# The opening stage of a decoder-trunk kernel: GpSimd subtractions moved, some work given to ScalarE and TensorE, a repacked modulation weight, a new order

## The chip, the cores and the metric

One Trainium2 chip, one core of it. The metric is the device time of one execution in microseconds (us). Every time below is either such a time or is read from one profiled execution. The engines are called by the profile's names: PE is TensorE (PEld its weight loads), DVE is VectorE, ACT is ScalarE, POOL is GpSimd, SP is SyncE, which here only issues transfers (SPq).

## What is computed

One decoder layer on 512 tokens of width 1024. The part that matters here is its beginning: a modulation vector from the condition `c`, a normalised and modulated input `h`, and the first projections of `h`.

```python
c_act = silu(c)
mod = c_act @ w_mod + b_mod                       # w_mod: 1024 x 6144
sh1, sc1, gt1, sh2, sc2, gt2 = split(mod, 6)
h = rms_norm(x, g_norm1) * (1 + sc1) + sh1        # x: 512 x 1024
proj = h @ w_in                                   # then gMLP, GLA, sparse attention, w_out
x = x + gt1 * mixer(proj)
h2 = rms_norm(x, g_norm2) * (1 + sc2) + sh2
out = x + gt2 * hier_moe(h2)                      # top-1 group, top-2 experts in it
```

Products are made to near-f32 accuracy from two parts: each operand is split into a high part (rounded to the fp32r type) and a low part (the operand minus its high part), and three products are added: high x high, high x low, low x high.

## The kernel before

The opening stage is everything up to the moment when the first six 128-column blocks of `w_in` have been multiplied with all of `h`. It is written out by hand as a list of steps, the string `START`. The loop over that string calls one small function for each word, so the string sets the order of the instructions on every engine; each engine then runs its own instructions strictly in that order and waits at the first one whose input is missing.

The width 1024 is cut into eight columns dc = 0 to 7 of 128. The words are, with the function that each calls:

- `Lx` (`load_xt`), `Lm` (`load_mod`), `Lu` (`first_load`): transfers, issued by SP in this order: four 128-token tiles of `x`; for each column a 1 MB piece of `w_mod` (the two 128-column pieces for the shift `sh1` and the scale `sc1`) in two transfers of 512 KB; six weight units of 512 KB, `raw`. There are four buffers for `w_mod` pieces and three for `raw`; a load whose buffer is still in use waits on SP, and all later loads wait behind it.
- `sq`, `rs`, `sc` (`x_sq`, `x_rstd`, `x_norm`): ACT squares a token tile and sums it, DVE and POOL make the reciprocal root, DVE scales the tile.
- `xt`, `xs`, `xe` (`x_t`, `x_evac`): PE transposes the tile in 128 x 128 pieces (`xs7` does the last column), and ACT or DVE copies a finished column out of PSUM into `xnT`.
- `mp`, `ma`, `mb` (`mod_products`, `mod_sums`): the modulation of a column. Partition p holds eight rows k = 0 to 7 of `w_mod`. ACT multiplies two of them with `c_act` into `mpg`; DVE adds the other six in two interleaved chains `macc` (SCALAR_TENSOR_TENSOR, 128 x 256 each) and joins the chains in one addition.
- `mo`, `mc` (`mod_column`, `mod_scale`): PE sums `macc` over the partitions by a product with a column of ones; DVE makes scale and shift `mc` of the column.
- `hh`, `hf`, `hl` (`h_hi`, `h_full`, `h_lo`): the modulated column. ACT writes its high part `hTh`; `hf` writes the full row in f32; `hl` subtracts to give the low part `hTl`. The letter in `hl0G` is the engine: V is DVE, G is POOL.
- `wh`, `wl` (`first_hi`, `first_lo`): high part (ACT) and low part (DVE or POOL, by the letter) of a weight unit; the low part of units 0 to 3 is `wlo`, of units 4 and 5 `mg`.
- `f` followed by unit, column and part (`first_c`): one product, 128 x 512. Each of the six units has 8 columns x 3 parts, so 144 products. Part 0 is hTh with the high weights, part 1 hTh with the low ones, part 2 hTl with the high ones.
- `wm` with a number (`warm`): that many dummy products on PE.

In the kernel before, the subtractions `wl0` to `wl3`, `wl5` (`wl4` is on DVE) and `hl0`, `hl1`, `hl4`, `hl6`, `hl7` carry the parts that are named G or V in the string; five of the weight subtractions and five of the `hl` subtractions run on POOL. After `START` come the next units (`gk`, then `av`), whose splits are ACT and DVE work, and then the rest of the layer, which is the same text in both kernels.

Of the kernel before, what the change touches and what calls it, by code (L numbers as in the profile page):

```python
# [38 lines left out]
LV = [1, 2, 4, 8, 16, 32, 64]  # L39

START = """
Lx0 Lx1 sq0 Lx2 rs0 sq1 Lx3 sc0 rs1 wm9 xt0 sq2 Lm0 sc1 rs2 sq3 xt1 sc2 rs3 xt2 Lu0 sc3 mp0 wm3 xt3 Lm1 ma0 xs7 xe0A
mb0 wh0 xe1A wl0G xe3A Lu1 xe4A xe2V wm10 mo0 mp1 mc0 Lm2 hf0 hh0 ma1 wh1 hl0G wm7 f000 mb1 f001 xe5A f100 xe7A wl1G
f102 f002 Lu2 xe6V mo1 mp2 mc1 Lu3 hf1 hh1 ma2 wm4 f101 wh2 hl1G f110 mb2 Lm3 f111 f010 f011 f200 f210 wh3 wl2G f202
f112 f212 f012 mo2 f300 mc2 f310 f302 Lu4 hf2 f312 hh2 wl3G f201 f211 mp3 hl2V f320 f120 f220 f121 ma3 f221 f322 Lu5
wh4 f020 f122 mb3 f301 f311 f321 f222 Lm4 f400 f410 f402 f420 f412 wh5 wl4V f021 mo3 f422 f022 wl5G f500 mc3 f510 f401
hf3 hh3 f502 f411 f520 f512 hl3V f330 f130 mp4 f230 f331 Lm5 f131 f501 ma4 f511 f430 f421 f530 mb4 f521 f231 f332 f030
f132 f522 f431 Lm6 f232 f531 f031 mo4 mp5 f432 mc4 f532 f032 hf4 hh4 ma5 hl4G f340 Lm7 mb5 f140 f240 f341 f141 f440
mp6 f540 f241 f342 f040 ma6 f142 mo5 f441 f242 mc5 f541 hf5 f041 hh5 f442 f542 mb6 f042 mp7 f350 f150 f250 f351 f151
f450 hl5V f550 mo6 f251 mc6 f050 f352 hf6 f152 hh6 f451 ma7 f252 f551 f051 hl6G f360 mb7 f160 f260 f361 f161 f460 f560  # L50
f261 f362 f060 f162 mo7 f452 mc7 f552 f461 hf7 f262 hh7 f561 f052 f061 f462 hl7G f370 f170 f270 f371 f171 f470 f570
f271 f372 f070 f172 f562 f471 f272 f571 f062 f071 f472 f572 f072
"""


# [116 lines left out]
def trunk(ctx: ExitStack, tc: tile.TileContext, I, out, dbg=None):  # L172
# [7 lines left out]
    V, A, G, T, SY = nc.vector, nc.scalar, nc.gpsimd, nc.tensor, nc.sync  # L180
# [21 lines left out]
    def bank(name="ms"):  # L202
        return (pmm if name == "mm" else pms).tile([128, 512], FT, name="bank_" + name)
# [4 lines left out]
    def big(tag, name, dt=FT, n=2048):  # L208
        return {"Y": mp, "YB": mp, "T1": bp, "T2": bp}.get(tag, bt_).tile([128, n], dt, name=name, tag=tag, bufs=BUFS[tag])
# [36 lines left out]
    wmr, first_raw = [], {}  # L246

    def load_mod(dc):
        t = big(("Y", "YB")[dc % 2], "wmod").rearrange("p (k h c) -> p k h c", k=8, h=2)
        a = I["w_mod"]  # L250
        for h in range(2):
            SY.dma_start(t[:, :, h, :], bass.AP(tensor=a.tensor, offset=a.offset + dc * 128 + 1024 * h,
                                                ap=[[8 * 6144, 128], [6144, 8], [1, 128]]))
        wmr.append(t)

    def load_unit(src, k):
# [1653 lines left out]
```

## Time and profile before

| | us |
|---|---|
| median of 3 runs | 804.54 (801.87 to 805.5) |
| the profiled execution | 802.08 |
| its span | 800.3 |
| PE busy in the span | 750.7 (94%) |
| DVE busy | 569.3 (71%) |
| ACT busy | 321.2 (40%) |
| POOL busy | 156.9 (20%) |

The span runs from the first instruction to the last; 1.8 us of the execution lie outside it. In the timeline a row is: start, duration, engine, line, operation, output<-inputs, count, and in brackets the idle time of the engine before it and what ended that. Instructions of one kind that follow each other are merged into one row, with their count behind x.

### The profile page before, as it was taken

Reading aid. Unit: us, or ns where it says so; the run is one execution under the profiler, and the core shown is the slowest. Engines: PE = TensorE matmul, PEld = TensorE weight load, DVE = VectorE, ACT = ScalarE, POOL = GpSimd, SP = SyncE. Lnnn points to the kernel's source line nnn. Section 1 sums busy time; section 2 is a strip of 40 time slices with the busy share of each in tenths; the row PEclk is TensorE's granted clock in tenths of the full one; section 3 lists DMA queues with packets and bytes.
Section 4 is the critical chain, followed back from the end, with each engine's and each line's share of the span. In section 5 each row is a group of like instructions: output and inputs, shape, how many; then the busy total and the mean of one; then the engine's idle time right before and its main releaser. Section 6 shows DMA issues by size and latency. Waiting matters only on the chain. (4 is left out here: it accounts for less than half of the span.)

```text
span 800.3 us, 11714 instructions
## 1 busy us (share of the span) xinstructions
PE 750.7 (94%) x4231; PEld 623.7 (78%) x4231; DVE 569.3 (71%) x1081; ACT 321.2 (40%) x573; POOL 156.9 (20%) x145
## 2 busy tenths in 40 slices
PE   7699998999999999999999999999999889899994
PEld 4477986998888889999788887889974567777773
DVE  5987737778748775865777677845467978777983
ACT  5434743241334224432244333433313445455761
POOL 2522207412121023330110041300000102212200
PEclk9799999999999999999999999999999999999998
DMA  9882144221212221257454576587566899999931
GB/s 303 255 262 90 57 135 140 79 79 53 80 54 79 79 80 53 71 196 257 146 161 148 168 244 202 183 284 228 181 216 218 274 338 343 370 313 362 365 67 27
DMA packets 67861, 144.88 MB, mean 181 GB/s; under 512 B 8349, under 2 KB 36146, under 8 KB 67546
## 3 DMA queue, kind: packets, MB, share of 16 engines
q1 hardware_dynamic: 59234, 130.00, 48.1%
q0 software_dynamic: 3024, 11.01, 5.6%
q10 hardware_dynamic: 5544, 3.10, 1.6%
q8 instruction: 34, 0.56, 0.3%
q14 instruction: 25, 0.20, 0.1%
HBM read 134.12 MB, written 11.29 MB: 182 GB/s over the span
## 5 line engine op out<-in xcount | busy, mean ns | idle before, releaser
L226 DVE TENSOR_TENSOR wlo<-raw,whi 128x1024 fp32r<-128x1024 f32 x70 | 91.7, 1313 | 55.9 <-ACT whi L225 55.2
L216 PE MATMUL bank_mm<-whi,hTh 128*128 128x256 f32 x352 | 100.8, 286 | 0.0
L216 PE MATMUL bank_mm<-wlo,hTh 128*128 128x256 f32 x352 | 98.8, 281 | 1.8 <-DVE wlo L226 1.8
L216 PE MATMUL bank_mm<-whi,hTl 128*128 128x256 f32 x352 | 98.8, 281 | 0.0
L216 PE MATMUL bank_mm<-hTh,whi 128*128 128x512 f32 x224 | 92.4, 413 | 0.0
L225 ACT ACTIVATE whi<-raw 128x1024 fp32r<-128x1024 f32 x70 | 73.2, 1054 | 46.4 <-DMA raw<-in_w_t_dram 27.5
L216 PE MATMUL bank_mm<-hTh,wlo 128*128 128x512 f32 x224 | 88.9, 397 | 0.0
L216 PE MATMUL bank_mm<-hTl,whi 128*128 128x512 f32 x224 | 88.4, 395 | 0.0
L216 PEld LDWEIGHTS bank_mm<-wlo,hTh 128*128 128x128 f32 x352 | 66.4, 189 | 2.2 <-DVE wlo L226 2.0
L216 PEld LDWEIGHTS bank_mm<-whi,hTh 128*128 128x128 f32 x352 | 66.4, 189 | 0.6 <-issue 0.3
L216 PEld LDWEIGHTS bank_mm<-whi,hTl 128*128 128x128 f32 x352 | 66.3, 188 | 0.0
L216 PEld LDWEIGHTS bank_mm<-hTh,whi 128*128 128x128 f32 x224 | 42.2, 188 | 11.1 <-issue 1.0
L216 PEld LDWEIGHTS bank_mm<-hTh,wlo 128*128 128x128 f32 x224 | 42.1, 188 | 10.5 <-DVE wlo L226 0.5
L216 PEld LDWEIGHTS bank_mm<-hTl,whi 128*128 128x128 f32 x224 | 42.1, 188 | 10.0 <-issue 0.7
L216 PE MATMUL bank_mm<-whi,mgs 128*128 128x256 f32 x256 | 49.7, 288 | 0.2 <-DVE mgs L229 0.2
L216 PE MATMUL bank_ms<-dnh,aT 128*128 128x512 f32 x120 | 44.5, 431 | 2.6 <-DVE aT L226 2.6
L963 DVE SCALAR_TENSOR_TENSOR acc<-raw,c_act,acc 128x1024 f32<-128x1024 f32 x28 | 39.0, 1404 | 8.2 <-DMA raw<-in_w_mod_dram 7.7
L216 PEld LDWEIGHTS bank_mm<-whi,mgs 128*128 128x128 f32 x256 | 40.8, 191 | 0.5 <-DVE mgs L229 0.4
L216 PE MATMUL bank_mm<-guh,XTh 128*128 128x512 f32 x88 | 39.1, 444 | 0.1
L216 PE MATMUL bank_mm<-gul,XTh 128*128 128x512 f32 x88 | 35.2, 401 | 1.8 <-DVE gul L226 1.8
L216 PE MATMUL bank_mm<-wlo,mgs 128*128 128x256 f32 x128 | 36.2, 282 | 0.0
L216 PE MATMUL bank_mm<-guh,XTl 128*128 128x512 f32 x88 | 35.4, 402 | 0.0
(453 smaller groups left out, 1739.3 us busy)
## 6 DMA issues: line engine op xcount, KB each, us to landing
raw<-in_w_t_dram SPq DMA_DIRECT2D x35, 512.0 KB
raw<-in_w_mod_dram SPq DMA_DIRECT2D x32, 512.0 KB
raw<-in_w_m_dram SPq DMA_DIRECT2D x24, 512.0 KB
raw_e<-in_w_ed_dram SPq DMA_DIRECT2D x22, 512.0 KB
wmod<-in_w_mod_dram SPq DMA_DIRECT2D x16, 512.0 KB
raw_x<-in_w_eg_dram SPq DMA_DIRECT2D x16, 512.0 KB
raw_x<-in_w_eu_dram SPq DMA_DIRECT2D x16, 512.0 KB
raw<-in_w_branch_dram SPq DMA_DIRECT2D x12, 512.0 KB
```

The costliest lines, as they stand in the source:

```text
L216: T.matmul(o, l[a], r[b], start=first and i == 0, stop=last and i == 2)
L225: A.activation(hi, src, AF.Copy)
L226: (eng or V).tensor_tensor(lo, src, hi.bitcast(FT), OP.subtract)
L963: V.scalar_tensor_tensor(acc[:, c], raw, c_act[:, kt:kt + 1], acc[:, c], OP.mult, OP.add)
```

## The change

- `w_mod` for the first two modulation vectors is also passed as a new array `w_ms`, packed so that partition p's data for a column is one run of 8 KB; each of its two transfers takes 4 KB of it (before: runs of 512 B). The first transfer holds rows k = 0 to 3, the second k = 4 to 7 (before: the shift half and the scale half).
- ACT makes rows k = 0, 1 (before 6, 7), DVE adds k = 2 to 7 (before 0 to 5). For columns 0 to 2 DVE stops at k = 5: rows 6 and 7 are multiplied with `c_act` on PE (`md`, `mod_direct`) into the same PSUM column. For columns 0 and 1 the two chains are not joined either: PE sums both. The join is a step of its own (`mj`) for the others.
- `hf` moves from DVE to ACT. All eight copies `xe` are on ACT (before two were on DVE).
- All `wl` and `hl` subtractions are on DVE; none is left on POOL.
- `START` is a new order. Its transfers stand in the same order as before.

```diff
 START = """
-Lx0 Lx1 sq0 Lx2 rs0 sq1 Lx3 sc0 rs1 wm9 xt0 sq2 Lm0 sc1 rs2 sq3 xt1 sc2 rs3 xt2 Lu0 sc3 mp0 wm3 xt3 Lm1 ma0 xs7 xe0A
...
+Lx0 Lx1 Lx2 Lx3 wm9 Lm0 Lu0 Lm1 Lu1 Lm2 Lu2 sq0 sq1 rs0 sc0 sq2 rs1 xt0 sq3 rs2 sc1 sc2 wm3 xt1 rs3 xt2 mp0 sc3 ma0
...
 def lay_out(a):
+    o["w_ms"] = f["w_mod"][0][:, 0:2048].reshape(128, 8, 2, 8, 128).transpose(3, 0, 1, 2, 4).reshape(8, 128, 2048)
...
     def load_mod(dc):
-        t = big(("Y", "YB")[dc % 2], "wmod").rearrange("p (k h c) -> p k h c", k=8, h=2)
-        a = I["w_mod"]
+        t = big(("Y", "YB")[dc % 2], "wmod")
         for h in range(2):
-            SY.dma_start(t[:, :, h, :], bass.AP(tensor=a.tensor, offset=a.offset + dc * 128 + 1024 * h,
-                                                ap=[[8 * 6144, 128], [6144, 8], [1, 128]]))
+            SY.dma_start(t[:, 1024 * h:1024 * h + 1024], I["w_ms"][dc][:, 1024 * h:1024 * h + 1024])
+        t = t.rearrange("p (k h c) -> p k h c", k=8, h=2)
...
+    DIRECT = {0: (6, 7), 1: (6, 7), 2: (6, 7)}
     def mod_products(dc):
...
-            A.activation(pg[:, i], wmr[dc][:, 6 + i], AF.Copy, scale=c_act[:, 6 + i:7 + i])
+            A.activation(pg[:, i], wmr[dc][:, i], AF.Copy, scale=c_act[:, i:i + 1])
...
+    def mod_join(dc):
+        acc = md_[dc][0]
+        V.tensor_tensor(acc[:, 0], acc[:, 0], acc[:, 1], OP.add)
+    def mod_direct(dc):
+        b = mb_[dc] = bank()
+        for i, k in enumerate(DIRECT[dc]):
+            for h in range(2):
+                T.matmul(b[:, h:h + 1], wmr[dc][:, k, h], c_act[:, k:k + 1], start=i == h == 0, stop=False)
...
     def mod_column(dc):
-        md = bank()
-        for h in range(2):
-            T.matmul(md[:, h:h + 1], md_[dc][0][:, 0, h], ones_c[:, 0:1].bitcast(FT), start=True, stop=True)
+        md = mb_.get(dc)
+        md = bank() if md is None else md
+        n = 2 if dc < 2 else 1
+        for i in range(n):
+            for h in range(2):
+                T.matmul(md[:, h:h + 1], md_[dc][0][:, i, h], ones_c[:, 0:1].bitcast(FT), start=dc not in mb_ and i == h == 0, stop=i == n - 1 and h == 1)
...
     def h_full(dc):
-        V.tensor_scalar(hf_[dc], xnT[dc // 4][:, dc % 4], mc_[dc][:, 1:2], mc_[dc][:, 0:1], OP.mult, OP.add)
+        A.activation(hf_[dc], xnT[dc // 4][:, dc % 4], AF.Identity, bias=mc_[dc][:, 0:1], scale=mc_[dc][:, 1:2])
```

On POOL, from the reciprocal roots of `x` to the first work after the stage, before:

```order
L221 TENSOR_TENSOR rstd_124<-rs_t,mhalf 128x1 x4
L277 TENSOR_TENSOR wlo<-raw,whi 128x1024
L361 TENSOR_TENSOR hTl<-hf,hTh 128x512
L277 TENSOR_TENSOR wlo<-raw,whi 128x1024
L361 TENSOR_TENSOR hTl<-hf,hTh 128x512
L277 TENSOR_TENSOR wlo<-raw,whi 128x1024 x2
L277 TENSOR_TENSOR mg_105<-raw,mg_104 128x1024
L361 TENSOR_TENSOR hTl<-hf,hTh 128x512 x3
```

and now:

```order
L222 TENSOR_TENSOR rstd_124<-rs_t,mhalf 128x1 x4
L422 MEMSET wg_629 32x256
L533 MEMSET gaug 32x512
L549 CAST mk<-tl_627 128x768
L624 TENSOR_TENSOR gm<-gm,ga 128x512 x2
```

The ten subtractions are gone from POOL; what follows the roots is the work after the stage.

On DVE, from the last scaled token tile to the second column's scale and shift, before:

```order
L308 TENSOR_SCALAR xb<-xb,rstd_124 128x1024
L335 SCALAR_TENSOR_TENSOR macc<-wmod,c_act,mpg 128x256 x2
L335 SCALAR_TENSOR_TENSOR macc<-wmod,c_act,macc 128x256 x4
L337 TENSOR_TENSOR macc<-macc 128x256
L321 COPY xnT_121<-bank_mm 128x512
L350 TENSOR_SCALAR mc<-bank_ms,bsc,pv 128x1
L351 TENSOR_SCALAR mc<-bank_ms,pv 128x1
L358 TENSOR_SCALAR hf<-xnT_121,mc 128x512
L335 SCALAR_TENSOR_TENSOR macc<-wmod,c_act,mpg 128x256 x2
L335 SCALAR_TENSOR_TENSOR macc<-wmod,c_act,macc 128x256 x4
L337 TENSOR_TENSOR macc<-macc 128x256
L321 COPY xnT_122<-bank_ms 128x512
```

and now:

```order
L308 TENSOR_SCALAR xb<-xb,rstd_124 128x1024
L338 SCALAR_TENSOR_TENSOR macc<-wmod,c_act,mpg 128x256 x2
L338 SCALAR_TENSOR_TENSOR macc<-wmod,c_act,macc 128x256 x2
L277 TENSOR_TENSOR wlo<-raw,whi 128x1024
L338 SCALAR_TENSOR_TENSOR macc<-wmod,c_act,mpg 128x256 x2
L366 TENSOR_SCALAR mc<-bank_ms,bsc,pv 128x1
L367 TENSOR_SCALAR mc<-bank_ms,pv 128x1
L338 SCALAR_TENSOR_TENSOR macc<-wmod,c_act,macc 128x256 x2
L277 TENSOR_TENSOR wlo<-raw,whi 128x1024
L366 TENSOR_SCALAR mc<-bank_ms,bsc,pv 128x1
L367 TENSOR_SCALAR mc<-bank_ms,pv 128x1
L338 SCALAR_TENSOR_TENSOR macc<-wmod,c_act,mpg 128x256 x2
```

A column's chain is two additions shorter and has no join, the copies and the full rows are gone, and a weight subtraction stands between the columns.

On ACT, from the first modulation rows to the first two high parts of `h`, before:

```order
L329 ACTIVATE mpg<-wmod,c_act 128x256 x2
L319 ACTIVATE xnT_121<-bank_ms 128x512
L274 ACTIVATE whi<-raw 128x1024
L319 ACTIVATE xnT_121<-bank_mm 128x512
L319 ACTIVATE xnT_121<-bank_ms 128x512
L319 ACTIVATE xnT_122<-bank_mm 128x512
L329 ACTIVATE mpg<-wmod,c_act 128x256 x2
L354 ACTIVATE hTh<-xnT_121,mc 128x512
L274 ACTIVATE whi<-raw 128x1024
L319 ACTIVATE xnT_122<-bank_ms 128x512 x2
L329 ACTIVATE mpg<-wmod,c_act 128x256 x2
L354 ACTIVATE hTh<-xnT_121,mc 128x512
```

and now:

```order
L319 ACTIVATE xnT_121<-bank_mm 128x512
L274 ACTIVATE whi<-raw 128x1024
L331 ACTIVATE mpg<-wmod,c_act 128x256 x2
L319 ACTIVATE xnT_121<-bank_mm 128x512
L319 ACTIVATE xnT_122<-bank_ms 128x512
L319 ACTIVATE xnT_121<-bank_ms 128x512
L274 ACTIVATE whi<-raw 128x1024
L370 ACTIVATE hTh<-xnT_121,mc 128x512
L331 ACTIVATE mpg<-wmod,c_act 128x256 x2
L374 ACTIVATE hf<-xnT_121,mc 128x512
L370 ACTIVATE hTh<-xnT_121,mc 128x512
L374 ACTIVATE hf<-xnT_121,mc 128x512
```

Two weight units now stand ahead of the first `hTh`, and each `hTh` is followed by its full row `hf`.

## Rows read from the trace of the kernel before

**Rows 1.** Stretches: length, then busy us (count) of PE, PEld, DVE, ACT, POOL

```profile
0.00:73.10 73.10, 58.54 (x242) 41.96 (x243) 57.35 (x103) 30.79 (x49) 25.02 (x24) 0.93 0.76 227
73.10:130.00 56.90, 56.80 (x343) 48.84 (x342) 30.66 (x45) 30.64 (x46) 9.78 (x11) 1.00 0.38 125
...
140.00:800.00 660.00, 628.91 (x3606) 527.34 (x3606) 471.30 (x926) 255.36 (x474) 112.29 (x106) 0.99 0.55 182
```

**Rows 2.** Timeline of PE: first product, two rows of a dense stretch, last product

```profile
20.08 0.50 PE L371 MATMUL bank_mm<-hTh,whi 128*128 128x512 f32 x1
...
47.56 1.56 PE L371 MATMUL bank_ms<-hTh,mg 128*128 128x512 f32 x6
...
48.96 0.40 PE L371 MATMUL bank_mm<-hTh,wlo 128*128 128x512 f32 x1
...
72.66 0.40 PE L371 MATMUL bank_mm<-hTl,whi 128*128 128x512 f32 x1
```

**Rows 3.** Groups by line, first 73.1 us: count, busy us, mean ns, idle before

```profile
L335 DVE SCALAR_TENSOR_TENSOR macc<-wmod,c_act,macc 128x256 f32<-128x256 f32 x32 | 23.8, 803 | 0.0
...
L277 POOL TENSOR_TENSOR wlo<-raw,whi 128x1024 fp32r<-128x1024 f32 x4 | 10.1, 2545 | 3.9 <-ACT whi L274 3.9
...
L361 POOL TENSOR_TENSOR hTl<-hf,hTh 128x512 fp32r<-128x512 f32 x5 | 7.6, 1527 | 27.4 <-ACT hTh L354 23.8 <-DVE macc L335 3.6
L337 DVE TENSOR_TENSOR macc<-macc 128x256 f32<-128x256 f32 x8 | 7.5, 939 | 0.3
```

**Rows 4.** Timeline of DVE and POOL, with and without POOL's subtractions beside it

```profile
28.13 6.91 DVE L335 SCALAR_TENSOR_TENSOR macc<-wmod,c_act,macc 128x256 f32<-128x256 f32 x4
...
29.31 5.05 POOL L277 TENSOR_TENSOR wlo<-raw,whi 128x1024 fp32r<-128x1024 f32 x2
...
43.42 1.21 DVE L277 TENSOR_TENSOR mg<-raw,mg 128x1024 fp32r<-128x1024 f32 x1
...
45.83 0.69 DVE L361 TENSOR_TENSOR hTl<-hf,hTh 128x512 fp32r<-128x512 f32 x1 [0.30 <-ACT hTh L354]
...
47.23 1.67 DVE L335 SCALAR_TENSOR_TENSOR macc<-wmod,c_act,macc 128x256 f32<-128x256 f32 x4
...
48.94 0.42 DVE L337 TENSOR_TENSOR macc<-macc 128x256 f32<-128x256 f32 x1
```

**Rows 5.** Timeline: what one step costs on ACT, on PE's column sums, on DVE

```profile
13.99 1.05 ACT L274 ACTIVATE whi<-raw 128x1024 fp32r<-128x1024 f32 x1
...
14.94 0.59 ACT L319 ACTIVATE xnT<-bank_mm 128x512 f32<-128x512 f32 x1
...
35.55 1.01 PE L342 MATMUL bank_ms<-ones_c,macc 128*128 128x1 f32 x4 [4.10 <-DVE macc L337]
...
43.84 0.50 PE L342 MATMUL bank_ms<-ones_c,macc 128*128 128x1 f32 x4
...
51.60 0.28 DVE L350 TENSOR_SCALAR mc<-bank_ms,bsc,pv 128x1 f32<-128x1 f32 x1 [2.24 <-PE bank_ms L342]
...
52.04 0.81 ACT L354 ACTIVATE hTh<-xnT,mc 128x512 fp32r<-128x512 f32 x1 [4.64 <-DVE mc L351]
...
52.76 0.90 ACT L329 ACTIVATE mpg<-wmod,c_act 128x256 f32<-128x256 f32 x2
```

**Rows 6.** Timeline: the fourth token tile's arrival, its scaling, the first copy from PSUM

```profile
8.87 1.06 ACT L302 ACTIVATE scr<-xb 128x1024 f32<-128x1024 f32 x1 [0.22 <-DMA xb<-in_x_dram]
...
11.27 0.75 DVE L308 TENSOR_SCALAR xb<-xb,rstd 128x1024 f32<-128x1024 f32 x1 [0.67 <-POOL rstd L221]
...
13.50 0.60 ACT L319 ACTIVATE xnT<-bank_ms 128x512 f32<-128x512 f32 x1
```

**Rows 7.** Stretches of 2 us; last: granted PE clock, DMA share, GB/s

```profile
28.00:30.00 2.00, 2.00 (x6) 1.61 (x6) 2.00 (x3) 1.64 (x2) 2.00 (x2) 0.50 0.35 139
...
44.00:46.00 2.00, 2.00 (x12) 1.67 (x12) 1.66 (x5) 1.02 (x2) 0.00 (x0) 1.00 1.20 290
...
52.00:54.00 2.00, 1.46 (x7) 0.90 (x6) 1.96 (x5) 1.61 (x3) 1.07 (x1) 1.00 1.05 434
```

More of the change, by code (lines that the diff above doesn't have):

```diff
@@ L41 @@
 START = """
-Lx0 Lx1 sq0 Lx2 rs0 sq1 Lx3 sc0 rs1 wm9 xt0 sq2 Lm0 sc1 rs2 sq3 xt1 sc2 rs3 xt2 Lu0 sc3 mp0 wm3 xt3 Lm1 ma0 xs7 xe0A
[L43 to L51, printed above, removed]
@@ L52 @@
-f271 f372 f070 f172 f562 f471 f272 f571 f062 f071 f472 f572 f072
+Lx0 Lx1 Lx2 Lx3 wm9 Lm0 Lu0 Lm1 Lu1 Lm2 Lu2 sq0 sq1 rs0 sc0 sq2 rs1 xt0 sq3 rs2 sc1 sc2 wm3 xt1 rs3 xt2 mp0 sc3 ma0
+wm3 xt3 mb0 xs7 xe0A xe2A md0 wh0 mo0 mp1 wl0V Lu3 Lm3 xe1A ma1 xe5A xe3A mc0 wh1 wm6 md1 mb1 hh0 wl1V Lu4 mo1 mp2
+f000 md2 mc1 hf0 ma2 f001 hh1 f100 hl0V f101 hf1 mb2 f010 f002 f102 wh3 f011 mj2 f110 f111 hl1V mo2 xe4A f300 wl3V wh2
+f302 f012 f112 f310 f312 mc2 mp3 f200 wl2V Lu5 Lm4 Lm5 Lm6 f202 f301 hh2 f210 f212 f311 ma3 hf2 f201 f211 f020 wh4 mb3
@@ new lines @@
+Lm7 f021 f120 f121 f220 xe6A f221 f320 f321 xe7A f400 mj3 f402 f410 hl2V mo3 wh5 f412 wl4V f022 f122 f222 f500 mp4 mc3
+f502 f401 wl5V f411 hh3 f510 f512 f322 f420 hf3 ma4 f421 f501 f511 f422 mp5 hl3V f520 f521 f522 mb4 f030 f031 f032
+f130 f131 f132 f230 mj4 f231 mp6 f232 ma5 mo4 f330 f331 mc4 f332 mb5 f430 hh4 f431 f432 f530 f531 hf4 f532 f040 f041
+mp7 mj5 f140 f141 ma6 mo5 f240 mc5 f241 f340 mb6 f341 hh5 f440 f441 f540 f541 hf5 f050 f051 f150 mj6 f151 f250 hl5V
+mo6 f251 hl4V f052 f152 mc6 f252 f042 ma7 f142 hh6 f242 f342 f442 mb7 hf6 f542 f350 f351 f352 f450 f451 f452 hl6V f550
@@ L53 @@
+f551 f552 mj7 f060 f061 mo7 f062 mc7 f160 f161 f162 hh7 f260 f261 f262 hf7 f360 f361 f362 f460 hl7V f461 f462 f560
+f561 f562 f070 f071 f072 f170 f171 f172 f270 f271 f272 f370 f371 f372 f470 f471 f472 f570 f571 f572
 """
@@ L334, in mod_sums @@
         for k in ks:
-            V.scalar_tensor_tensor(acc[:, k % 2], wmr[dc][:, k], c_act[:, k:k + 1], pg[:, k] if k < 2 else acc[:, k % 2], OP.mult, OP.add)
-        if 5 in ks:
-            V.tensor_tensor(acc[:, 0], acc[:, 0], acc[:, 1], OP.add)
-    def mod_column(dc):
-        md = bank()
-        for h in range(2):
-            T.matmul(md[:, h:h + 1], md_[dc][0][:, 0, h], ones_c[:, 0:1].bitcast(FT), start=True, stop=True)
+            if k not in DIRECT.get(dc, ()):
+                V.scalar_tensor_tensor(acc[:, k % 2], wmr[dc][:, k], c_act[:, k:k + 1], pg[:, k - 2] if k < 4 else acc[:, k % 2], OP.mult, OP.add)
+    def mod_join(dc):
+        acc = md_[dc][0]
+        V.tensor_tensor(acc[:, 0], acc[:, 0], acc[:, 1], OP.add)
+    mb_ = {}
+    def mod_direct(dc):
[3 more added lines that the diff above has]
+                T.matmul(b[:, h:h + 1], wmr[dc][:, k, h], c_act[:, k:k + 1], start=i == h == 0, stop=False)
+    def mod_column(dc):
+        md = mb_.get(dc)
[4 more added lines that the diff above has]
+                T.matmul(md[:, h:h + 1], md_[dc][0][:, i, h], ones_c[:, 0:1].bitcast(FT), start=dc not in mb_ and i == h == 0, stop=i == n - 1 and h == 1)
         md_[dc] = md
```

2 lines of the change are left out of this document (1 added, 1 removed).

## The prediction

> **What bounds the kernel now.** I read the stretches first [rows 1]. After 73.1 us PE is the bound: 56.80 of the next 56.90 us are busy, and 628.91 of the 660 from 140 on. In the first 73.1 us it is not: 58.54 us look busy, but the stage's real work is 144 products, and the dense stretch in the timeline of PE [rows 2] shows their pace: six that begin at 47.56 are followed by the next at 48.96, so 1.40 / 6 = 0.233 us each, 33.6 us in all. The first starts at 20.08, the last at 72.66 and ends at 73.06. So 53.0 us pass for 33.6 us of products and a few column sums; some 15 us are waits or half-speed products. The kernel after the stage is the same text and is full of PE work, so what the stage ends earlier should come out of the total.
>
> What PE waits for is the next column's modulation, which is DVE's chain. Four additions take 1.67 us and a join 0.42 when POOL is quiet; beside two of POOL's subtractions (29.31, 5.05 us) four take 6.91 [rows 4]. By the groups [rows 3] the 32 additions took 23.8 us where 32 x 0.42 = 13.4 would do, and the 8 joins 7.5 where 8 x 0.42 = 3.4 would: 14.5 us of DVE time are lost beside nine subtractions on POOL of 2.55 and 1.53 us (a tenth, on another tile, is alike). PE loses twice: it idles 4.10 us ahead of the sum at 35.55, and that sum then takes 1.01 us where 0.50 is normal [rows 5], since the clock has fallen to 0.50 of full speed [rows 7].
>
> **The change, part by part.** *Subtractions from POOL to DVE.* DVE gets five of 1.21 us and five of 0.69 [rows 4], 9.5 us, and gets back 14.5. It also gives up eight full rows, two copies, six additions and two joins. What is left from 12.0 on (the fourth tile scaled, 11.27 + 0.75 [rows 6]): 42 additions x 0.42 + 6 joins x 0.42 + 6 weight subtractions x 1.21 + 8 row subtractions x 0.69 + 8 x 0.44 for scale and shift (51.60 to 52.04 [rows 5]) = 36.5 us. In the second half a column costs DVE 7 x 0.42 + 0.44 + 0.69 = 4.1 us, and PE 18 x 0.233 + 0.50 = 4.7. So DVE is no longer the bound there; its slack of 0.6 us a column is the cover.
>
> *Work to ACT.* ACT gets eight full rows at the pace of `hTh` (52.04 to 52.76, 0.72 us) and two copies of 0.6 [rows 5]. A full row in f32 has no row of its own on ACT; its bounds are the PSUM copy's 0.59 and the 0.81 of `hTh`, and I take 0.72 because size, bias and scale are those of `hTh`. ACT then has 8 x 0.90 + 8 x 0.55 + 6 x 0.95 + 16 x 0.72 = 28.8 us in the stage, but packed: in my walk it has no free moment from the first copy to about 31 us. There ACT sets the pace.
>
> *Terms on the array.* Two rows of one column are four products of one column of data. The nearest row is the column sum: two such products 0.50 us [rows 5], so 1.0 us per column on PE, and the column sums of the first two columns grow from 0.50 to 1.0. They cost PE 3 x 1.0 + 2 x 0.5 = 4.0 us and save DVE 3.4. If a product against raw weights cost nothing more than its bare pass, it might be half (0.5); at the low clock double (2.0).
>
> *w_mod in long rows.* While only w_mod moves, in 512 B runs, the rate is 290 GB/s; with weight units of 4 KB per partition in flight it is 434 [rows 7]. 512 KB then take 1.2 us instead of 1.8. The x tiles arrive as before, the last at 8.87 [rows 6]. From there at 1.25 us apiece: column 0 at 10.1 and 11.4, unit 0 at 12.6, column 1 at 13.9 and 15.1, unit 1 at 16.4, column 2 at 17.6 and 18.9. ACT reaches them later than that, so little of this gain is seen. The Trainium skill (DMA: Bandwidth & Descriptors, Specifications) sets the limit for line rate at 512 B and so speaks against any gain from longer rows; the 290 against 434 GB/s of the trace disagree. By that rule column 2's second half and units 3 and 4 would come up to 1.4 us after they are wanted, and the end would lie 1.4 us later than below.
>
> *The order, walked.* Up to the fourth tile nothing changes. Three dummies now stand between the first two tiles' transposes, which I price at 0.4 us: the first copy starts at 13.9 instead of 13.50 [rows 6]. Then ACT runs without pause: two copies 1.1, unit 0's high part 0.95, column 1's products 0.9, two copies 1.1: 17.95. The six dummies on PE need a bank that these copies free: 6 x 0.233 to 19.4. Behind them stand the direct terms and the sum of column 1, 2 x 1.0: 21.4. Only then comes the first product, 1.3 us later than before. From there PE has 33.6 + 1.0 (column 2's direct terms) + 6 x 0.50 (sums) = 37.6 us. Where the walk makes it wait: 0.6 us for unit 2's low part (its high part is at 25.95 on ACT, DVE ends the subtraction at 28.4), and some 0.1 us each at the joins of columns 2, 3, 4 and at the low part of column 3: together 1.0. The end of the stage: 21.4 + 37.6 + 1.0 + 0.2 for the last product's tail = 60.2, against 73.06.
>
> *Queues.* SP's order is the same. Unit 5's load, with columns 4 to 7 behind it, waits for unit 2's subtraction, 28.4. A transfer takes 1.2 us alone, and at most 4.0 more if all of 8.87 - 4 x 1.2 at the start were latency [rows 6]; I take 31.0, in time for the 32.8 at which PE wants it split; at 33.6 it would cost 1.8. POOL now runs only the roots, so the two clears for the next stage no longer stand behind subtractions. The next units' splits on ACT and DVE (`gk`, `av`) come some 5 us ahead of the stage's end, as before.
>
> **Sum.** 73.06 - 60.2 = 12.9 us. From the profiled execution, 802.08 - 12.9 = 789.2; from the median, 804.54, it is 791.6. I name 790.5.
>
> **Rivals.** *The clock falls in the thin stretch.* Between the last transposes (about 14.8) and the dense products (about 22.7) PE has only one-column products, idle time and 1.4 us of dummies. For it: idle stretches of this stage were followed by a granted clock of 0.50 [rows 7], which is 1.2 instead of 2.4 GHz, and the sum at 35.55 after 4.10 us of idling took double. Against: the dummies, and the weight loads of the small products. Price: dummies +1.4, column 1's terms and sum +2.0, column 2's terms +1.0, some eight products +0.23 each until it recovers, 1.9: 6.3 us, gain 6.6, so 795.5 to 798. The Trainium skill (TensorE: Matmul & The Clock Gate, Part 1) has the low clock as the default, which only activity lifts; the rows at 28 and 35.55 agree.
>
> *The gain is given back later.* The next stages would meet transfers or splits that are not 13 us earlier. Against: nothing that PE waits for after 73 is a transfer, and 56.80 of 56.90 us are busy. It would end within 4 us of now, 800 to 803.
>
> *The change makes it slower.* One mechanism: the small pieces between products keep PE at 0.50 through the stage. Each product then costs 0.233 more, all 144 33.6 us, and the total is about 21 us longer than before, some 824. It decides from 12.9 / 0.233 = 55 products at half clock on; below that the change still gains. Against: DVE and ACT no longer leave gaps of several us.
>
> *Better than the walk.* If the bank wait and the direct terms cost half, the first product starts near 19.5 and the stage ends at 58: 788, or 785.5 from a quick run.
>
> **How the numbers follow.** Forecast 0.62, clock 0.20, given back 0.08, slower 0.05, better 0.05. The forecast's own span is 787 to 793 (the ends of the full-row price, 16 x 0.1, of the load, 1.8, and the spread of the runs, 801.87 to 805.5). The range reaches down to the better case and up over the clock's: 786 to 799, leaving out the given-back and the slower case and tails. A measurement of this kernel tells 0.5%, 4 us, from no change. Faster by more: 0.62 + 0.05 + nearly all of 0.20 + a little of 0.08 = 0.88. Within: 0.07. Slower: 0.05.
>
> **What the changed profile would show.** No subtraction on POOL before 60 us; four additions 1.7 us and joins 0.42 throughout; first product near 21.4, last near 60; ACT without idle time from 14 to 31; over 400 GB/s while columns 0 to 2 load. Wrong if the first product starts after 24, if granted clocks under 1.00 stand between 15 and 30, if PE waits for `hTh` or `hTl` in columns 4 to 7 (then ACT or DVE is the new bound), or if the stage ends at 60 and the total has not moved by as much.

## The result and the profile after

| | before | after |
|---|---|---|
| median of 6 runs | 803.2 (799.18 to 805.5) | 792.98 (789.76 to 795.75) |
| profiled execution | 802.08 | 794.46 |
| its span | 800.3 | 792.8 |
| first product of the stage | 20.08 | 21.64 |
| first product of the next stage (`gk`) | 72.90 | 62.14 |
| POOL busy | 156.9 | 135.1 |

The ratio of the times is 0.9856, with a 95% interval from 0.9819 to 0.9893: 10.2 us less by the medians. I call the start of the first `gk` product the stage's end; in the profiled executions it moved by 10.76 us. Line numbers differ from before: products are now L387, column sums L358, terms on the array L350, dummies L396, additions L338, joins L342, `hTh` L370, `hf` L374, `hTl` L377. Everything after the stage is the same text.

Stretches of the kernel after (length, then busy us and count of PE, PEld, DVE, ACT, POOL, then granted PE clock, DMA share, GB/s), in answer to [rows 1] and [rows 7]:

```profile
0.00:62.30 62.30, 57.34 (x261) 45.81 (x263) 43.80 (x98) 39.63 (x63) 5.36 (x14) 0.89 0.74 280
62.30:119.20 56.90, 56.79 (x344) 49.06 (x344) 29.59 (x44) 28.26 (x42) 9.93 (x11) 1.00 0.35 111
129.20:789.20 660.00, 630.85 (x3606) 529.10 (x3606) 472.37 (x926) 255.35 (x474) 110.00 (x106) 0.99 0.55 182
...
14.00:16.00 2.00, 1.94 (x19) 1.87 (x18) 0.73 (x1) 2.00 (x5) 0.00 (x0) 1.00 1.03 422
16.00:18.00 2.00, 0.90 (x4) 0.48 (x5) 2.00 (x7) 2.00 (x5) 0.00 (x0) 1.00 1.02 408
18.00:20.00 2.00, 2.00 (x12) 1.83 (x10) 1.61 (x2) 2.00 (x5) 0.00 (x0) 0.57 1.03 412
20.00:22.00 2.00, 2.00 (x10) 2.00 (x10) 0.18 (x1) 0.62 (x1) 0.00 (x0) 0.50 1.02 408
...
28.00:30.00 2.00, 2.00 (x10) 1.72 (x11) 1.35 (x3) 0.92 (x2) 0.00 (x0) 0.86 0.97 303
```

After the stage PE is as full as it was. Inside it the clock is at half speed (1.2 of 2.4 GHz) from about 18.3 to 28.5, and "busy 2.00" there hides slow work. POOL is busy for 5.36 us of the stage, and the transfers run at 408 to 422 GB/s from 14 to 22.

Timeline of PE after (start, duration, count; in brackets the idle time before), in answer to [rows 2] and to the column sums of [rows 5]:

```profile
14.10 0.95 PE L350 MATMUL bank_ms<-c_act,wmod 128*128 128x1 f32 x8
14.91 1.03 PE L358 MATMUL bank_ms<-ones_c,macc 128*128 128x1 f32 x8
17.05 1.53 PE L396 MATMUL bank_ms<-wmm 128*128 128x512 bf16 x5 [1.11 <-ACT xnT L319]
18.37 1.71 PE L350 MATMUL bank_ms<-c_act,wmod 128*128 128x1 f32 x8
...
19.94 1.84 PE L358 MATMUL bank_ms<-ones_c,macc 128*128 128x1 f32 x8
21.64 0.77 PE L387 MATMUL bank_mm<-hTh,whi 128*128 128x512 f32 x1
22.22 1.70 PE L350 MATMUL bank_ms<-c_act,wmod 128*128 128x1 f32 x8
23.78 0.77 PE L387 MATMUL bank_mm<-hTh,wlo 128*128 128x512 f32 x1
...
27.76 0.85 PE L358 MATMUL bank_ms<-ones_c,macc 128*128 128x1 f32 x4
28.47 0.51 PE L387 MATMUL bank_ms<-hTh,whi 128*128 128x512 f32 x1
...
34.43 0.50 PE L358 MATMUL bank_ms<-ones_c,macc 128*128 128x1 f32 x4
34.79 0.48 PE L387 MATMUL bank_ms<-hTl,mg 128*128 128x512 f32 x1
...
62.14 0.39 PE L217 MATMUL bank_ms<-hTh,gk_hl 128*128 128x512 f32 x1
```

Column 0's terms and sum take 0.95 and 1.03 us, column 1's, after 1.11 us of waiting and six dummies (the trace holds five of them), 1.71 and 1.84: the same instructions at half the clock. The 1.11 us is PE's only wait from there to the end of the stage. In the kernel before, its list of waits (total, times, longest) has for the joins alone:

```profile
PE bank_ms L342 <- DVE macc L337: 10.0, 5, 4.1
```

Groups by line in the first 62.3 us after (count, busy us, mean ns, idle before), in answer to [rows 3], and four rows of its DVE and ACT timelines, in answer to [rows 4] and [rows 6]:

```profile
L338 DVE SCALAR_TENSOR_TENSOR macc<-wmod,c_act,macc 128x256 f32<-128x256 f32 x26 | 11.5, 501 | 0.0
L374 ACT ACTIVATE hf<-xnT,mc 128x512 f32<-128x512 f32 x8 | 6.4, 804 | 0.0
L377 DVE TENSOR_TENSOR hTl<-hf,hTh 128x512 fp32r<-128x512 f32 x8 | 5.4, 684 | 1.6 <-ACT hf L374 1.6
L277 DVE TENSOR_TENSOR wlo<-raw,whi 128x1024 fp32r<-128x1024 f32 x4 | 4.9, 1221 | 1.5 <-ACT whi L274 1.4
L342 DVE TENSOR_TENSOR macc<-macc 128x256 f32<-128x256 f32 x6 | 2.5, 423 | 0.2
```

```profile
30.89 1.67 DVE L338 SCALAR_TENSOR_TENSOR macc<-wmod,c_act,macc 128x256 f32<-128x256 f32 x4
...
13.20 0.60 ACT L319 ACTIVATE xnT<-bank_ms 128x512 f32<-128x512 f32 x1 [2.05 <-PE bank_ms L314]
...
22.32 0.81 ACT L370 ACTIVATE hTh<-xnT,mc 128x512 fp32r<-128x512 f32 x1 [1.70 <-DVE mc L367]
...
29.09 0.82 ACT L370 ACTIVATE hTh<-xnT,mc 128x512 fp32r<-128x512 f32 x1 [2.07 <-DVE mc L367]
```

The additions are at 501 ns mean (803 before), the joins at 423 (939 before). ACT has two pauses of 1.70 and 2.07 us, each for a scale and shift that waits for a column sum on PE, which comes late at the low clock.

### The profile page after: what moved, and what is told of

It is laid out like the page before. It is cut to its first block, busy times and chain, and to the rows that moved or that the text cites. A ratio compares the mean times of both kernels' runs of the same rounds, so it can differ in the third digit from the quotient of the medians.

```text
span 792.8 us, 11741 instructions
## 1 busy us (share of the span) xinstructions
PE 751.3 (95%) x4250; PEld 629.4 (79%) x4251; DVE 555.7 (70%) x1073; ACT 327.6 (41%) x583; POOL 135.1 (17%) x135
## 5 line engine op out<-in xcount | busy, mean ns | idle before, releaser
L227 DVE TENSOR_TENSOR wlo<-raw,whi 128x1024 fp32r<-128x1024 f32 x70 | 93.7, 1343 | 57.2 <-ACT whi L226 57.0
L226 ACT ACTIVATE whi<-raw 128x1024 fp32r<-128x1024 f32 x70 | 73.2, 1054 | 48.9 <-DMA raw<-in_w_t_dram 31.1
```

Source lines behind the costliest of these rows:

```text
L226: A.activation(hi, src, AF.Copy)
L227: (eng or V).tensor_tensor(lo, src, hi.bitcast(FT), OP.subtract)
```

## The experiments

All twelve in one table. "Products" is the time from the first product to the stage's end, "rest" the profiled execution less the stage's end. The totals are medians, beside the median of the kernel before in the same set of runs.

| kernel | first product | products | stage end | rest | total | before | ratio (95%) |
|---|---|---|---|---|---|---|---|
| before | 20.08 | 52.8 | 72.90 | 729.2 | | 803.2 | |
| after | 21.64 | 40.5 | 62.14 | 732.3 | 792.98 | 803.2 | 0.986 (0.982 to 0.989) |
| e1 | 25.48 | 41.4 | 66.86 | 732.6 | 798.29 | 804.86 | 0.992 (0.989 to 0.995) |
| e2 | 18.93 | 45.7 | 64.59 | 731.8 | 796.59 | 804.86 | 0.990 (0.985 to 0.994) |
| e3 | 24.51 | 40.2 | 64.68 | 731.1 | 796.01 | 804.86 | 0.991 (0.987 to 0.994) |
| e4 | 22.39 | 37.5 | 59.85 | 731.7 | 788.05 | 804.86 | 0.979 (0.976 to 0.982) |
| e5 | 19.16 | 52.8 | 71.96 | 729.2 | 802.17 | 803.62 | 0.998 (0.996 to 1.001) |
| e6 | 20.32 | 39.6 | 59.95 | 730.9 | 794.46 | 803.62 | 0.988 (0.984 to 0.992) |
| e7 | 20.12 | 39.6 | 59.73 | 728.7 | 790.27 | 803.62 | 0.984 (0.980 to 0.988) |
| e8 | 20.20 | 40.3 | 60.52 | 735.5 | 792.53 | 803.62 | 0.986 (0.982 to 0.990) |
| e9 | 19.72 | 38.9 | 58.66 | 732.2 | 791.35 | 802.83 | 0.986 (0.982 to 0.989) |
| e10 | 20.45 | 39.2 | 59.62 | 732.0 | 791.86 | 802.83 | 0.987 (0.984 to 0.991) |
| e11 | 17.96 | 45.6 | 63.51 | 733.8 | 796.80 | 802.83 | 0.991 (0.988 to 0.994) |
| e12 | 20.40 | 37.9 | 58.34 | 729.8 | 789.34 | 803.13 | 0.983 (0.981 to 0.985) |

The rest, the same work in every kernel, spreads over 728.7 to 735.5 us. So a total says little about a stage that differs by two microseconds; the stage's own times are what is compared.

These times are of one execution each, and they differ ahead of every edit, too. The steps up to the first copy out of PSUM are the same in the kernel after and in its variants (e3 differs there only in its transfers), yet that copy starts at 12.71 us in e7, at 13.20 in the kernel after, at 14.06 in e3, 14.29 in e1 and 14.88 in e4: the transposes ahead of it stand 0.11 us apart in e7 and 0.21 in e4 from 10 to 15.5. Counted from that copy to the stage's end, the kernel after takes 48.9 us, e1 52.6, e3 50.6, e4 45.0, e6 46.5, e7 47.0, e8 46.3, e9 45.6, e10 46.2 and e12 45.0; in the old order before takes 59.4, e2 51.4, e5 59.2 and e11 50.8.

**e1_pool_back: the subtractions on POOL again.** Only words of the kernel after's `START` change:

```diff
-wl0V wl1V wl2V wl3V wl5V hl0V hl1V hl4V hl6V hl7V
+wl0G wl1G wl2G wl3G wl5G hl0G hl1G hl4G hl6G hl7G
```

> The changed kernel with the ten subtractions (low parts of units 0, 1, 2, 3, 5 and of columns 0, 1, 4, 6, 7) back on POOL; all else as changed. Theory (DVE's additions are held up beside POOL's subtractions, and that set the stage): additions and joins of 2 us and more come back, PE waits for column sums, the stage ends at 68 to 73 us and the total is 799 to 803. Rival (the new order, the full rows on ACT and the terms on the array are the gain): the stage ends by 64 and the total stays at 793 to 795.

The total is 5.3 us above the kernel after's, the stage ends 4.7 us later; both lie between the theory and the rival. DVE and POOL in its timeline:

```profile
16.75 2.67 DVE L338 SCALAR_TENSOR_TENSOR macc<-wmod,c_act,mpg 128x256 f32<-128x256 f32 x2 [2.76 <-ACT mpg L331]
...
19.66 2.96 DVE L338 SCALAR_TENSOR_TENSOR macc<-wmod,c_act,macc 128x256 f32<-128x256 f32 x2
...
16.40 2.35 POOL L277 TENSOR_TENSOR wlo<-raw,whi 128x1024 fp32r<-128x1024 f32 x1 [4.77 <-ACT whi L274]
19.59 2.35 POOL L277 TENSOR_TENSOR wlo<-raw,whi 128x1024 fp32r<-128x1024 f32 x1 [0.84 <-ACT whi L274]
```

POOL's subtractions end at 18.75 and 21.94, the two pairs of additions beside them at 19.42 and 22.62: 0.67 and 0.68 us behind, where a pair alone takes 0.88. The additions stood nearly still until POOL was done. The Trainium skill (SBUF — State Buffer, Who interferes with whom) describes this as an exclusive lock between a VectorE instruction with two SBUF inputs and a GpSimd one that reads SBUF; the two ends agree. Of the 4.7 us, 1.1 are there at the first copy, ahead of POOL's first subtraction. PE then waits 2.77 us for DVE ahead of its dummies, where the kernel after waits 1.11: 1.7 us. The other 2 us or so are dummies and products at half clock, which lasts from 19.9 to about 33.5 here and from 18.3 to 28.5 there. So the loss beside POOL is 1.7 us directly and at most 3.6 with the clock, not the whole gain; that the new order meets POOL less often is likely, but not shown.

**e2_before_dve: that part alone.** The kernel before, with the same ten letters G turned to V.

> The kernel before with only the ten subtractions moved from POOL to DVE, in the old order. Theory: DVE gets 9.5 us and gets back 14.5, so the stage ends about 5 us earlier, at 66 to 69, and the total is 797 to 799. Rival (the gain needs the new order): DVE, already the engine that is waited for, only gets more work, and the total is 802 to 808.

The stage ends at 64.59, 8.3 us earlier than before, 7.2 of them after the first product. Its group of additions, in answer to [rows 3]:

```profile
L335 DVE SCALAR_TENSOR_TENSOR macc<-wmod,c_act,macc 128x256 f32<-128x256 f32 x32 | 13.9, 497 | 0.0
```

23.8 us have become 13.9, and PE's waits for the joins 2.0 us in place of 10.0. This one edit, in the old order, makes about three quarters of the 10.76 us, more than its own expectation allowed; here DVE still does all the full rows and sums.

**e3_short_rows: the kernel after with 512 B runs of w_mod.** The edit also gives back the old halves (shift, then scale), so that ACT's first rows of a column wait for both transfers and not for one; the run doesn't separate the two.

```diff
-            SY.dma_start(t[:, 1024 * h:1024 * h + 1024], I["w_ms"][dc][:, 1024 * h:1024 * h + 1024])
+            SY.dma_start(t[:, :, h, :], bass.AP(tensor=a.tensor, offset=a.offset + dc * 128 + 1024 * h,
+                                                ap=[[8 * 6144, 128], [6144, 8], [1, 128]]))
```

> The changed kernel with w_mod read as before, in runs of 512 B. Theory: the pieces arrive 0.6 us later each, which costs 1.4 us at most: 793 to 795. Rival (the transfers were the bound): each of the eight columns comes over 1 us later, PE waits, and 4 us or more are lost: 797 or more.

The stage ends 2.5 us later, 796.01 us in total is beyond the theory's 795, and all of the 2.5 us arises ahead of the first product (24.51 against 21.64). Its stretches from 8 to 24 and, from its list of waits (total, times, longest), the one that grew, and its dummies; then the same stretches of the kernel after:

```profile
8.00:16.00 8.00, 8.00 (x48) 6.87 (x47) 4.08 (x9) 4.62 (x9) 1.75 (x3) 1.00 1.15 314
16.00:24.00 8.00, 5.56 (x27) 4.42 (x27) 4.44 (x8) 5.71 (x11) 0.00 (x0) 0.73 1.11 345
...
ACT mpg L332 <- DMA wmod<-in_w_mod_dram: 11.8, 8, 2.7
...
19.18 2.26 PE L397 MATMUL bank_ms<-wmm 128*128 128x512 bf16 x5 [2.38 <-ACT xnT L320]
```

```profile
8.00:16.00 8.00, 7.94 (x53) 6.70 (x51) 4.72 (x10) 5.60 (x12) 1.85 (x3) 0.79 1.02 399
16.00:24.00 8.00, 6.90 (x31) 6.21 (x32) 5.79 (x15) 6.30 (x12) 0.00 (x0) 0.64 1.03 408
```

ACT waits 11.8 us for `w_mod`, against 1.9 in the kernel after, but little of it is on the path. Of the 2.87 us ahead of the first product, 0.86 are there at the first copy; 1.27 are PE's longer wait for a bank ahead of its dummies (2.38 us against 1.11), behind ACT's wait of 1.16 us for column 1; and 0.73 are dummies at half clock, since the clock fell at about 19.7, among them. So the short rows and old halves together cost 1.3 us directly, within the theory's 1.4. (The granted clock of 1.00 in the first of these rows is not to be relied on: up to 12.7 e3's transposes stand 0.21 us apart, as they do in the kernel after at 0.50.)

**e5_before_long_rows: the packed w_mod alone, in the kernel before.**

> The kernel before with only the packed w_mod (rows of 8 KB, two transfers of 4 KB a partition). Theory (beside POOL's subtractions DVE sets the stage, so earlier data wait for DVE): the stage ends at 72 to 73 and the total is within 1.5 us of the kernel before. Rival (the rows are worth by themselves what their removal cost in the changed kernel, 2.5 us of the stage): the stage ends near 70.5 and the total is 2 to 4 us shorter.

The rate in the same two stretches rises from 316 and 344 to 402 and 386 GB/s, but the stage ends only 0.94 us earlier and the total cannot be told from before. There the next column waits for DVE beside POOL, not for its weights. Long rows pay only once the additions are quick.

**e4_more_dummies: hold the clock.** `wn` is `wm` with a PSUM bank from the other pool, so that the dummies don't wait for a copy.

```diff
-md0 wh0 mo0 mp1 wl0V Lu3 Lm3 xe1A ma1 xe5A xe3A mc0 wh1 wm6 md1 mb1 hh0 wl1V Lu4 mo1 mp2
+md0 wh0 mo0 wn10 mp1 wl0V Lu3 Lm3 xe1A ma1 xe5A xe3A mc0 wh1 md1 wn3 mb1 hh0 wl1V Lu4 mo1 mp2
```

> The changed kernel with ten dummy products between the sum of column 0 and the direct terms of column 1 (in place of six that waited for a later bank) and three between those terms and the sum of column 1. Theory (the stage's lateness against 60 us is the clock, which fell to 0.50 from 18.3 to 28.5): the granted clock stays at 1.00 there, the stage ends at 59 to 60.5 although 0.7 us of dummies are on the path, and the total is 789 to 791 with runs closer together. Rival (the lateness is ACT's and DVE's chain, and the clock only follows): the stage ends at 62 to 63 and the total is 793 to 794.

Timeline of PE and two of its stretches:

```profile
17.97 2.32 PE L396 MATMUL bank_mm<-wmm 128*128 128x512 bf16 x9
20.13 0.95 PE L350 MATMUL bank_ms<-c_act,wmod 128*128 128x1 f32 x8
...
22.39 0.48 PE L387 MATMUL bank_mm<-hTh,whi 128*128 128x512 f32 x1
22.71 0.95 PE L350 MATMUL bank_ms<-c_act,wmod 128*128 128x1 f32 x8
```

```profile
18.00:20.00 2.00, 1.95 (x10) 0.93 (x12) 2.00 (x7) 2.00 (x5) 0.00 (x0) 1.00 1.02 406
22.00:24.00 2.00, 2.00 (x16) 1.92 (x16) 1.43 (x5) 1.24 (x3) 0.00 (x0) 1.00 0.98 311
```

The clock stays at 1.00 from 15.7 to the end of the stage, the terms take 0.95 us each time, and the products need 37.5 us where the kernel after needs 40.5. The stage ends at 59.85, as its theory said. Its median is 788.05, 1 us under the theory's range, 16.8 us below before in its set, and the lowest of all.

**e8_no_dummies: the kernel after without its six dummies.** The word `wm6` is taken out.

> The changed kernel without the six dummy products ahead of column 1's direct terms. Theory (the stretch is too thin for the high clock even with them): the first product starts up to 1.4 us earlier, the granted clock falls as before or sooner and stays at 0.50 as long, the stage ends within 1.5 us of 62.1 either way, total 792 to 795. Rival (the dummies hold the clock in a good part of the runs): without them the stage ends at 63.5 or later and the total is 795 to 797.

The stage ends at 60.52, 1.6 us before the kernel after's, and the total is 792.53, within the theory's range: as placed, the six dummies gain nothing. The clock falls with them (18.3 to 28.5) and without them (19.9 to 26.7).

**e7_no_direct: the terms on DVE again.** All `md` words go, and

```diff
-    DIRECT = {0: (6, 7), 1: (6, 7), 2: (6, 7)}
+    DIRECT = {}
```

> The changed kernel without the direct terms on PE: DVE adds rows 2 to 7 for columns 0 to 2 as well, the column sums of columns 0 and 1 still take both chains. Theory (in this stretch PE is the bound, and at the low clock the one-column products cost double, 1.7 us a column): 3.4 us leave PE's path, DVE gets 2.5 us beside it, the stage ends at 59 to 60.5, total 789.5 to 791.5. Rival (the terms save DVE time that is on the path): the stage ends 1 to 2.5 us later, total 794 to 796.

The stage ends at 59.73, the total is 790.27, both as its theory said. But here the clock was low only from 16.2 to 19.6, ahead of the first product, so part of the 2.4 us is that. The next two separate it.

**e9_dummies_no_direct and e12_dummies_through: both, with few and with many dummies.** e9 is e7 with `wn10` after `mo0` in place of `wm6`; e12 is e9 with

```diff
-mo0 wn10 mp1
+mo0 wn15 mp1
...
-mo1 mp2
+mo1 wn3 mp2
```

> The changed kernel with ten dummies of a bank of their own after the first column sum, and all additions of the modulation on DVE and ACT (no direct terms on the array). Theory: the two gains add, since the dummies hold the clock at 1.00 from about 16 us and the direct terms cost the array about 4 us for 2.5 us of DVE; stage end 57.5 to 59, total 786 to 788. Rival: with the clock held DVE is the bound and wants the relief; stage end 60 or later, total 790 or more.

> The kernel without direct terms (e9_dummies_no_direct), with fifteen dummies in place of ten after the first column sum and three more after the second, so that the array has no pause of over half a microsecond between the transposes and the first product. Theory: the clock then holds at 1.00 from 16 us to the end of the stage, which ends at 57.5 to 58.5, and the total follows it: 787 to 790. Rival: the last microseconds of the stage don't reach the total (in e10_dummies_rows_dve the clock held and the stage ended early, yet its total was that of the changed kernel); stage end 58 or so, but total 791 to 793.

e9's stage ends at 58.66 as expected, but PE pauses 1.21 us ahead of column 1's sum and 0.61 ahead of the product at 21.50, and its clock is low from about 21 to 24; its total, 791.35, is the rival's. In e12 the first of these pauses is 0.30 us, and the second is not there. The same two stretches of e9, then of e12:

```profile
20.00:22.00 2.00, 1.39 (x5) 0.69 (x4) 2.00 (x7) 1.90 (x3) 0.00 (x0) 0.75 1.03 412
22.00:24.00 2.00, 2.00 (x6) 1.47 (x5) 1.97 (x6) 2.00 (x4) 0.00 (x0) 0.50 1.03 410
```

```profile
20.00:22.00 2.00, 1.96 (x9) 1.07 (x8) 2.00 (x6) 1.90 (x4) 0.00 (x0) 1.00 1.01 403
22.00:24.00 2.00, 1.64 (x6) 0.86 (x5) 1.97 (x6) 2.00 (x4) 0.00 (x0) 1.00 1.04 416
```

e12 holds the clock, ends the stage at 58.34, the earliest of all, and takes 789.34 us, as its theory said. With the clock held, the products of e12 need 37.9 us and those of e4, with the terms on the array, 37.5: the terms neither help nor hurt by more than half a microsecond there. (e12 has no terms on PE, but waits 0.61 us for DVE's join of column 2.) e4's later end comes from its beginning: its clock was low from 8.9 to 15.7, and its last transposes start at 16.05 where e12's start at 14.01. From the first copy on, both take 45.0 us.

**e6_rows_on_dve and e10_dummies_rows_dve: the full rows on DVE again**, once in the kernel after and once in e4:

```diff
-        A.activation(hf_[dc], xnT[dc // 4][:, dc % 4], AF.Identity, bias=mc_[dc][:, 0:1], scale=mc_[dc][:, 1:2])
+        V.tensor_scalar(hf_[dc], xnT[dc // 4][:, dc % 4], mc_[dc][:, 1:2], mc_[dc][:, 0:1], OP.mult, OP.add)
```

> The changed kernel with the full rows back on DVE (0.55 us each there). Theory (from the first product on PE is the bound and DVE has some 0.6 us of slack per column): DVE gets 3.8 us in the stage, most of it hidden, the stage ends at 61 to 63.5, total 792 to 795. Rival (ACT's packed stretch from 14 to 31 us is the bound): ACT is relieved of 0.8 us per column, the stage ends 1.5 us or more earlier than the changed kernel's 62.1, total 790 to 791.

> The kernel with more dummies (e4_more_dummies), but the full rows on DVE again. Theory: DVE has the 3 us to spare, the stage still ends at 59.5 to 61.5 and the total is 788 to 790, so that the place of the full rows is worth a microsecond at most. Rival: ACT's rows are needed, DVE is late for the low parts in the second half, stage end 62 or later and total 792 or more.

e6 ends its stage at 59.95, as the rival said, and its total, 794.46, is the theory's. Its clock was low for 3.4 us only (22.2 to 25.6), so its profile says nothing of the rows. But it says something of the clock, for up to the first product its steps on PE are those of the kernel after:

```profile
17.32 1.46 PE L396 MATMUL bank_ms<-wmm 128*128 128x512 bf16 x5 [1.11 <-ACT xnT L319]
18.62 0.95 PE L350 MATMUL bank_ms<-c_act,wmod 128*128 128x1 f32 x8
19.43 1.03 PE L358 MATMUL bank_ms<-ones_c,macc 128*128 128x1 f32 x8
```

After the same 1.11 us of waiting and the same dummies, column 1's terms and sum take 0.95 and 1.03 us, not 1.71 and 1.84, and the first product starts at 20.32. So when the clock falls there differs from one execution to the next.

In e10 the clock holds from about 12 on, as in e4 from 15.7, and the products need 39.2 us where e4's need 37.5. The wait behind it, from e10's list for 20.4 to 59.6:

```profile
PEld bank_ms L358 <- DVE macc L342: 2.5, 6, 0.8
```

In e4 this wait is 0.5 us in two. So ACT's rows are worth about 1.7 us from the first product on, and 1.2 from the first copy on; e10's stage end, 59.62, is the theory's, but its total, 791.86, is above the theory's 790, and I can't show that the rows are worth as much in the total.

**e11_dve_and_rows: the old order with DVE's subtractions and long rows.**

> The kernel before with the old order, with two of the parts: all subtractions on DVE and the packed w_mod. Theory: the two parts make most of the change; stage end 61.5 to 63.5 and total 793 to 795, so that the new order, ACT's rows and copies and the terms on the array together add 2 us at most. Rival: in the old order the packed weight adds nothing to the subtractions moved, stage end 64.5 or later and total 796 to 797, and the rest of the change is worth some 4 us.

The stage ends at 63.51, the upper edge of the theory's range, 1.1 us before e2's; the total, 796.8, is the rival's. In the old order the first product comes earlier (17.96), but the products take 45.6 us. The new order with ACT's rows and copies cuts that to 40.5, or 37.5 to 37.9 with the clock held, and pays for it with a later start: from the first copy on, e11 takes 50.8 us, the kernel after 48.9, and e4 and e12 45.0.

## Why the prediction was right, and where it was not

The forecast of 790.5 us (787 to 793) has the measured median, 792.98, at its upper end, and 10.2 us of the 12.9 came. The mechanism is the one named: additions slowed beside POOL, gone when POOL's subtractions go. e2 shows it alone (8.3 us of stage), e1 the other way round (additions that stop beside POOL again, 1.7 us of waiting and at most 3.6 with the clock). The rival's mechanism came as well: the granted clock was under 1.00 between 15 and 30, which the forecast had named as a sign of being wrong. That the median still lies in the forecast's span, and not in the rival's 795.5 to 798, is in part luck, as the sum below shows.

- **First product, 21.4 foreseen, 21.64 measured**, but by two misses that nearly cancel. The first copy starts at 13.20, not 13.9, though it is a matter of the execution (12.71 to 14.88 above), and the six dummies are done at 18.37, not 19.4. Column 1's terms and sum then take 18.37 to 21.64, 3.27 us, not 2.0.
- **End of the stage's last product, 60.2 foreseen, 62.30 measured** (the first `gk` product starts at 62.14). The step that failed is the weighing of forecast and clock rival: the clock did fall in the thin stretch. Over the walk's prices it cost 1.3 us on column 1 (above), and after the first product 0.35 on that product, 0.56 on column 2's terms (22.22 to 23.78, 1.56 us where the walk had 1.0), 1.9 on nine products (23.78 to 27.76, where 9 x 0.233 = 2.1 would do) and 0.3 on the next sum and the product behind it (27.76 to 28.82): 4.4 us. The rival said 6.3; its 1.4 for dummies at half clock did not arise, since the clock fell only as they ended. Three terms of my walk were too high: the start by 1.0; the waits of 1.0, which are not there; and the other five sums, which with the slower product behind each take 0.45 us (34.43 to 35.11, less one product) and not 0.50, together 0.25. 60.2 + 4.4 - 2.3 = 62.3. So the stage came out near the forecast because overpriced terms paid for half of what the clock cost. e4 and e12, where the clock holds, need 37.5 and 37.9 us from the first product to the first `gk` product; the walk had 38.6.
- **The clock rule.** The Trainium skill (TensorE: Matmul & The Clock Gate, Part 1) makes the low clock the default that activity lifts. The stretch at 16 to 18, with 0.90 us of PE work, is followed by 0.57 and 0.50, which agrees; in e6 the clock held through the same pause, to 22.2. The fences of e9 and e12 show the same place with and without pauses.
- **Long rows.** "Little of this gain is seen" was priced at nothing; the runs show at most 1.3 us on the path. My walk had ACT's own pace as the limit from 13.9 on; with short rows ACT waits for the first three columns in a row (2.44, 1.16 and 0.90 us in e3), and 1.3 us of that reach the first product. The rest of e3's later stage end is its later first copy and its clock. The 512 B that the Trainium skill (DMA: Bandwidth & Descriptors, Specifications) takes as enough for line rate were not enough here: 314 against 399 GB/s in the fences of e3; the measurement decides.
- **Work to ACT.** The full row was priced well: the next ACT instruction starts 0.71 us later (23.04 to 23.75) for a foreseen 0.72. "No free moment to 31" is wrong: the pauses of 1.70 and 2.07 us above come mostly from the clock; e4 and e12, which hold it, wait for a scale and shift only once up to 31, for 0.77 and 0.73 us.
- **Terms on the array.** 0.81 us at full clock and 1.56 at half lie within the bounds 0.5 and 2.0. Taken away (e7) the stage is no later; their use is not shown by any run.
- **Queues.** Unit 5 is split at 32.41 without a wait for its load, 32.8 was foreseen. PE waits for no `hTh` or `hTl` in columns 4 to 7.
- **A slip in the better case.** With the stage's end at 58, the quick run of 801.87 would give 786.8, not 785.5.
- **Given back later.** In the two profiles shown, the lead shrinks from 10.76 us at the end of the stage to 7.5 us at the end. e7 has the same text behind the stage and loses nothing. Two stretches of the kernel after, then two at the same place of e7:

```profile
126.00:130.00 4.00, 1.64 (x15) 1.45 (x14) 3.35 (x5) 0.24 (x1) 3.57 (x3) 1.00 0.46 144
...
132.00:134.00 2.00, 2.00 (x12) 2.00 (x11) 1.14 (x4) 0.00 (x0) 1.19 (x1) 0.50 0.41 147
```

```profile
123.00:127.00 4.00, 1.64 (x16) 1.45 (x14) 3.64 (x5) 1.06 (x1) 3.86 (x3) 1.00 0.46 142
...
129.00:131.00 2.00, 2.00 (x21) 2.00 (x19) 1.44 (x4) 0.63 (x2) 1.50 (x1) 1.00 0.29 66
```

Both have the same pause of PE (1.64 us of work in 4), and the clock falls in one and not in the other. e7's lead is 13.2 us at the end of the stage and 13.7 at the end; e12's 14.6 and 13.9. By the medians, 10.2 us of the total stand against the 10.8 of the stage. Over the kernel after and the twelve experiments the gain of the total is on average 0.7 us less than that of the profiled stage, single ones lying from 3.8 us below to 3.8 above; so nothing of the size of this rival is given back.

What stays open: whether e4 (0.976 to 0.982) and e12 (0.981 to 0.985) are truly below the kernel after (0.982 to 0.989) in the total. Their medians are 5 and 4 us lower and their stages end 2.3 and 3.8 us earlier, but the intervals touch, they ran in other sets, and e10 held the clock and ended its stage as early as e4 without the lower total. The granted clock of all runs, over the whole execution, speaks for them: on average 0.988 in e4 (0.985 to 0.992) and 0.989 in e12 (0.986 to 0.992), against 0.983 in the kernel after (0.977 to 0.987). In e10 it is 0.985 (0.981 to 0.988), and its profiled run is one of the two highest. So a held clock is not one execution's luck in e4 and e12, and may be in e10.

## What to carry to other kernels

When an engine's instructions take several times their usual time, look for what runs beside them before counting work: giving the faster engine more work can end its stage earlier. Price the stretch ahead of a dense phase at both levels of the clock, and fill pauses there with dummies that depend on nothing. A faster transfer shows only after the consumer has stopped being the limit, so test it in the new order too. Before a stage's end is compared between two profiles, look whether they differ ahead of the edit.

## What was not expected of the hardware

- Two additions beside a 2.35 us POOL subtraction took 2.67 and 2.96 us where 0.88 is normal, and ended 0.67 and 0.68 us after it: nearly a full stop, not a slower pace.
- The clock fell at about 18.3, as six dummies ended, after 1.8 us of one-column products and 1.1 us of waiting; in e6, after the same, only at 22.2. With ten and three dummies (e4), or fifteen and three (e12), and no pause of over 0.3 us between the transposes and the first product, the granted clock stayed at 1.00.
- After the same pause of PE further on, the clock fell in one execution and not in another (0.50 at 132 in the kernel after, 1.00 in e7). What decides it no run here shows.
